# A streaming encoder block with mixture of experts: a new order of its front, 27 weight slots, sums in PSUM, late down biases, overflow loads on POOL's queue

## The chip, the cores and the metric

The kernel runs on one core of a Trainium2 chip. The metric is the device time of one execution in microseconds (us); a statement about a kernel rests on the median of its runs. Engines are named as in the profile: PE (TensorE), PEld (its weight loads), DVE (VectorE), ACT (ScalarE), POOL (GpSimd), SP (SyncE, which issues most DMA transfers here).

## What is computed

One block over 256 tokens of width 1024, float32: a projection, two attention mixers, a gated merge, a norm, then a mixture of 32 experts, four to a token, and a second norm.

```
proj = x @ w_in -> qa, ckv, qi, ki, wi, qb, kb, vb, ga, gb
y_a = sparse_indexed_attention(qa, rms_norm(ckv), qi, layer_norm(ki), wi, w_uk, w_uv)   # top 64 keys
y_b = chunk_band_attention(qb, kb, vb, rel_bias)
merged = sigmoid(ga) * (y_a @ w_branch_a) + sigmoid(gb) * (y_b @ w_branch_b)
x = layer_norm(DN_ALPHA * x + merged @ w_out)
logits = x @ w_router + b_router;  gates = softmax(top 4 of 32)
for each expert e and its tokens:
    h = (clip(x @ w_up[e] + b_up[e]) + 1) * swish(min(x @ w_gate[e] + b_gate[e], 7))
    y += gate * (h @ w_down[e] + b_down[e])
x = layer_norm(DN_ALPHA * x + y)
```

The weights of the experts are 3 x 4 MB each, so 12 loads of 1 MB to an expert and 384 of the kernel's 408 loads.

## The kernel before

**Slots.** SBUF is kept as 25 slots of 128 x 2048 float32 (1 MB). `slot()` takes one, `free()` and `done()` count it back; the buffer itself is free when the last reader has ended. All weights come through a list in the order of their use (L95 to L125): `load_next` (L78) takes a slot and issues one load on SP's queue, `pump(reserve)` (L86) issues loads as long as more than `reserve` slots stay free. SP issues in program order and waits at each load until its buffer is free. Beside the loads the slots hold x and its halves, scores, gates, and in the expert loop x1, wa, wb, wc (work tiles), acc (the sums) and, from the fourth to the 21st expert, the down biases.

**The front** (to L727). Products of the projections, branches and w_out run on halves: `ahead(n)` (L187) splits the first n chunks of 1 MB, each into a rounded high part (ACT, two activations) and the rest as low part (two subtractions on the engine that `LO_ENGINE` names, V for DVE or G for POOL), into two slots. `AHEAD` says how many chunks are split ahead of use and `RESERVE` what each pump leaves free. `project_T(g)` and `project(g)` run the three products of the halves for group g of two chunks; `used()` frees a chunk and pumps. The order before: B's queries and keys (groups 0, 1) with the indexer's scores and top-k on DVE, A's queries (2), B's scores and softmax, v of B (3), A's scores and softmax, gate A (4), `attend` B, gate A (5), `attend` A, gate B (6, 7), the branches A then B, w_out, norm, router. `exps` takes the maxima on DVE and the exponentials on ACT by head, `normalise` scales by head on DVE, `attend` turns the weights by PE transposes and then multiplies with v.

**The experts** (L931). For expert e: `run_gate_up(e)`, copies to SBUF, `run_down(e - 1)`, every second time the gather and gates of the next pair, `act_fn(e)`, and after every second expert `combine`, which multiplies a pair's rows back to the tokens in two fresh PSUM banks and adds them to acc on DVE. Four products open the sums in PSUM before the last expert (L963). `down_biases` (L895) runs at e = 3. At e = 20 `overflow` (L823) branches on the largest count of an expert's tokens; its body isn't entered with these inputs. The loads pumped behind the down of expert 19 go out on POOL's queue.

Of the kernel before, what the change touches and what calls it, by code (L numbers as in the profile page):

```python
# [15 lines left out]
NT = 2  # L16
D = 1024
KD = 8
H = 8
NE = 32  # L20
CAP = 64
TOPK = 64
# [26 lines left out]
def body(nc, tc, slots, sm, psp, xT_d, x_d, w_g0, w_qi, w_in, ikgb_d, wuk_d,  # L49
# [4 lines left out]
    # ---------------------------------------------------------------- slots and loads  # L54
# [42 lines left out]
    for i in range(2):  # L97
        plan(("ba", i), wba_d[i])
        plan(("bb", i), wbb_d[i])
# [27 lines left out]
    # ---------------------------------------------------------------- first loads  # L127
# [16 lines left out]
    ikgb = sm.tile([128, 3], F32, name="ikgb")  # L144
    SP.dma_start(ikgb, ikgb_d)
# [9 lines left out]
    epst = sm.tile([128, 1], F32, name="epst")  # L155
# [14 lines left out]
    # ---------------------------------------------------------------- exact halves of float32 operands  # L170
# [12 lines left out]
    order = [("in", i) for i in range(16)] + [("ba", 0), ("ba", 1), ("bb", 0), ("bb", 1)] + [("wo", i) for i in range(4)]  # L183
    IN, BA, BB, WO = 0, 16, 18, 20
    halves = []

    def ahead(n):  # L187
        """splits the first n chunks of that order"""
# [10 lines left out]
    def part(i, which, k, per):  # L199
        """row block k of chunk i"""  # L200
# [18 lines left out]
    def warm(n):  # L219
        """keeps the tensor engine's clock up while it waits"""  # L220
# [34 lines left out]
    def project(g, sink):  # L255
        """group g of the input projections, token-major"""
# [13 lines left out]
    def project_T(g, sink):  # L270
        """group g of the input projections, feature-major; two row blocks share a bank, so only the first starts it"""
# [21 lines left out]
    # k_idx layer norm and c_kv rms norm, token-major  # L293
# [26 lines left out]
    def head_scores(qT, kT, tb, sink):  # L320
        """pairs of heads lie on the two halves of the partitions"""
# [14 lines left out]
    # ---------------------------------------------------------------- B queries and keys, the indexer  # L336
# [51 lines left out]
    # ---------------------------------------------------------------- A queries  # L388
# [11 lines left out]
    V.memset(sB[1][0:64, :, 192:256], NEG)  # L400

# [3 lines left out]
    def exps(s, w, tb):  # L405
        V.tensor_reduce(mx[:, w, tb, :], s[tb], axis=AX.X, op=ALU.max, negate=True)
        for h in range(H):
            A.activation(s[tb][:, h, :], s[tb][:, h, :], AF.Exp, bias=mx[:, w, tb, h:h + 1],
                         accum_out=sums[:, w, tb, h:h + 1])

    def normalise(s, w, tb):
        V.reciprocal(sums[:, w, tb, :], sums[:, w, tb, :])
        for h in range(H):
            V.tensor_scalar(s[tb][:, h, :], s[tb][:, h, :], sums[:, w, tb, h:h + 1], None, op0=ALU.mult)
# [7 lines left out]
    for tb in range(NT):  # L422
        head_scores(qbT, lambda j: kbT[:, j, :], tb, score_sink(sB))
        exps(sB, 1, tb)
    free(1)
    sa0_s = slot("sa0_vb")
    sa1_s = slot("sa1")
    sA = [sa0_s[:, 0:1024].rearrange("p (h s) -> p h s", h=8), sa1_s.rearrange("p (h s) -> p h s", h=8)]
    for tb in range(NT):
        sl = slice(KOFF[tb], KOFF[tb] + KEYS[tb])  # L430
        for h in range(H):
            V.scalar_tensor_tensor(sA[tb][:, h, :], negd[:, sl], 2.0 ** -(h + 1), amask[:, sl],
                                   op0=ALU.mult, op1=ALU.add)
    free(1)
    vb = sa0_s[:, 1024:2048].rearrange("p (b c) -> p b c", b=2)
    project(3, lambda tb, p: acopy(vb[:, tb, :], p))
    normalise(sB, 1, 0)
    normalise(sB, 1, 1)
    for tb in range(NT):
        head_scores(qaT, lambda j: kaT[:, j, :], tb, score_sink(sA))  # L440
        exps(sA, 0, tb)
    free(2)

    y_s = [slot("yA"), slot("yB")]
    yHL = [[t[:, o:o + 1024].rearrange("p (j t) -> p j t", j=4) for o in (0, 1024)] for t in y_s]

    def attend(s, v, w):
        pts = [slot("pt0"), slot("pt1")]
        pT = [t[:, 0:1536].rearrange("p (b h t) -> p b h t", b=3, h=4) for t in pts]
        for j2 in range(2):  # L450
            for bi, (tb, sb) in enumerate(((0, 0), (1, 0), (1, 1))):
# [3 lines left out]
                (vcopy if bi != 1 else acopy)(pT[j2][:, bi, :, :].rearrange("p h t -> p (h t)"), p)  # L455
        for j2 in range(2):
            o = bank("pv")
            for jj in range(2):
                for tb in range(NT):
                    for sb in range(tb + 1):  # L460
                        for par in range(2):
# [3 lines left out]
                                      v[:, sb, h * 64:(h + 1) * 64], pT[j2][:, tb + sb, i, :],  # L465
                                      start=(sb == 0), stop=(sb == tb), skip_group_check=True)
            hi, lo = [t[:, 2 * j2:2 * j2 + 2, :] for t in yHL[w]]
# [3 lines left out]
    sg_s = [slot("sgA"), slot("sgB")]  # L471
    sg = [s.rearrange("p (k t) -> p k t", k=KD) for s in sg_s]

    def gate_sink(w, n):
        return lambda js, p: A.activation(sg[w][:, 4 * n + js.start:4 * n + js.stop, :], p, AF.Sigmoid)

    project_T(4, gate_sink(0, 0))
    attend(sB, vb, 1)
    free(2)
    normalise(sA, 0, 0)  # L480
    normalise(sA, 0, 1)
    project_T(5, gate_sink(0, 1))
    attend(sA, va, 0)
    free(3)
# [5 lines left out]
    mg = sg[1]  # L490
# [18 lines left out]
    yHL = [[t.bitcast(F32R) for t in hl] for hl in yHL]  # L509

    def branch(w, c, ps):
        """chunk c of a branch's rows; at the last one the gate and, for B, the sum of the two and its halves"""
        for f in range(KD):
# [10 lines left out]
            if w:  # L524
# [5 lines left out]
    for c in range(2):  # L530
        ahead(BA + c + 1 + AHEAD[BA + c])
        branch(0, c, ps)
# [5 lines left out]
    for c in range(2):  # L538
        ahead(BB + c + 1 + AHEAD[BB + c])
        branch(1, c, ps)  # L540
# [8 lines left out]
    def norm_apply(tb, groups):  # L549
        """z = (x1 - mean) * rstd, and x1 = z * g + b"""  # L550
# [38 lines left out]
    def route_sums(copy=vcopy):  # L589
        """the router's products by experts, in four sums over two row blocks each"""  # L590
# [7 lines left out]
    def route(tb):  # L598
        """the router's logits (the norm's gain in the weights, its offset in the row), and which experts a token takes"""
# [9 lines left out]
    def count_up(tb):  # L609
        """the place of each token among an expert's tokens; far off for the tokens that it doesn't take"""  # L610
# [11 lines left out]
    sgm = wa_s[:, 1536:1792].rearrange("p (j s) -> p j s", j=4)  # L622

# [38 lines left out]
    # the second token tile's last columns in two halves, for a shorter way from their sums to the norm  # L662
# [66 lines left out]
    # ---------------------------------------------------------------- experts  # L729
# [9 lines left out]
    def combine_weights(pt, gated):  # L739
        """pt = the gated one-hot rows turned, from their two halves of 64 columns for each token tile"""  # L740
# [6 lines left out]
    def dispatch_weights(g):  # L747
        """for the pair g of experts"""
# [39 lines left out]
    def down(hT, wd):  # L788
        """the halves of the columns on the halves of the partitions"""
# [7 lines left out]
    def rows_of(e, p, first=0, size=512):  # L797
        """an expert's rows to its half of the pair's partitions"""
# [3 lines left out]

    def combine(g):
# [7 lines left out]
    def add(tb, ps):  # L811
        for n in range(2):
# [273 lines left out]
```

## Time and profile before

| | us |
|---|---|
| three runs, median (lowest to highest) | 1157.8 (1157.16 to 1158.95) |
| span of the profiled execution | 1156.1 |
| PE busy in it | 1067.6 (92%) |
| DVE, ACT, POOL busy | 351.9, 227.6, 85.5 |
| moved by DMA | 437.51 MB, 378 GB/s on average |

The profile lists one execution. Busy shares are averages over stages with different limits; the stretches further down separate them. "Idle before ... <-X" names what ended an engine's idle time, a `q` behind an engine its instruction queue. L numbers are lines of the kernel before.

### The profile page before, as it was taken

To read this page: it belongs to the slowest core of one execution; us is meant where nothing else is said; L and a number is where in the kernel's file an instruction comes from. 1 tells how busy PE (TensorE), PEld (TensorE's weight loads), DVE (VectorE), ACT (ScalarE), POOL (GpSimd) and SP (SyncE) were. 2 spreads that over 40 slices of the span, in tenths; PEclk is the share of its full clock that TensorE was granted. 3 is DMA by queue.
4 is the path that set the end of the run, shared out by engine and by line. 5 is a ranking of instruction groups with operands and counts; after the bars stand their busy time and mean duration, and the time that the engine had idled before them with its cause. 6 is when DMAs were issued, how large, how long until landed. Compare 5 with 4: busy or idle time off the path is not lost. (4 is left out here: it accounts for less than half of the span.)

```text
span 1156.1 us, 13824 instructions
## 1 busy us (share of the span) xinstructions
PE 1067.6 (92%) x5599; PEld 540.9 (47%) x5599; DVE 351.9 (30%) x811; ACT 227.6 (20%) x424; POOL 85.5 (7%) x60
## 2 busy tenths in 40 slices
PE   8997899999899999999899999996699999999896
PEld 8987899634244443434343434341243434343432
DVE  6797826412212322121212121210212121212124
ACT  3645342221011111111111111110011111111112
POOL 4113723000000000000000000001000000000001
PEclk9997999999899999999999999998799999999998
DMA  8940747999999999999999999999989999999995
GB/s 335 382 154 1 280 180 306 359 420 422 407 405 421 421 420 421 421 421 421 421 421 421 421 422 421 421 422 422 418 353 421 421 421 421 421 421 421 421 421 189
DMA packets 63932, 437.51 MB, mean 378 GB/s; under 512 B 7252, under 2 KB 7892, under 8 KB 11892
## 3 DMA queue, kind: packets, MB, share of 16 engines
q1 hardware_dynamic: 61270, 421.61, 88.5%
q0 software_dynamic: 1728, 12.58, 2.6%
q10 hardware_dynamic: 864, 2.36, 0.6%
q8 instruction: 46, 0.75, 0.3%
q14 instruction: 24, 0.20, 0.0%
HBM read 435.48 MB, written 1.05 MB: 378 GB/s over the span
## 5 line engine op out<-in xcount | busy, mean ns | idle before, releaser
L761 PE MATMUL gu<-ld,wa 128*64 128x512 f32 x1024 | 458.9, 602 | 27.3 <-DMA ld<-in_dram 23.4
L759 PE MATMUL gu<-ld,wa 128*64 128x512 f32 x1024 | 457.9, 601 | 7.5 <-DVEq L832 6.8
L793 PE MATMUL y<-ld,wc 128*64 128x512 f32 x992 | 240.4, 606 | 19.7 <-DMA ld<-in_dram 19.7
L759 PEld LDWEIGHTS gu<-ld,wa 128*64 128x64 f32 x1024 | 136.7, 138 | 241.0 <-issue 221.4
L780 DVE TENSOR_TENSOR wc<-tr,wb 128x256 f32<-128x256 f32 x64 | 27.0, 422 | 669.7 <-PE tr L776 669.7
L761 PEld LDWEIGHTS gu<-ld,wa 128*64 128x64 f32 x1024 | 136.2, 138 | 93.2 <-DMA ld<-in_dram 46.4
L793 PEld LDWEIGHTS y<-ld,wc 128*64 128x64 f32 x992 | 77.4, 138 | 169.6 <-issue 131.2
L175 ACT ACTIVATE wb<-gu 128x512 f32<-128x512 f32 x64 | 38.3, 598 | 442.6 <-PE gu L761 234.5
L175 ACT ACTIVATE wc<-y 64x512 f32<-64x512 f32 (+1 forms) x66 | 38.3, 580 | 239.8 <-PE y L793 234.1
L279 PE MATMUL fm<-xh,hi 128*128 128x256 f32 x224 | 66.4, 297 | 9.7 <-ACT sa_vb L175 5.4
L635 PEld LDWEIGHTS ga<-wa,x 128*128 128x128 f32 x512 | 61.6, 196 | 12.4 <-issue 12.2
L180 POOL TENSOR_TENSOR lo<-ld,hi 128x1024 fp32r<-128x1024 f32 x24 | 59.0, 2491 | 97.7 <-ACT hi L175 72.4
L279 PE MATMUL fm<-xl,hi 128*128 128x256 f32 x224 | 65.2, 291 | 0.0
L279 PE MATMUL fm<-xh,lo 128*128 128x256 f32 x224 | 65.1, 291 | 0.0
L635 PE MATMUL ga<-wa,x 128*128 128x128 f32 x512 | 64.8, 285 | 0.0
L808 PE MATMUL c<-wc,wb 128*128 128x512 f32 x120 | 54.0, 592 | 0.0
L83 POOL DMA_DIRECT2D ld<-in_dram x12 | 6.7, 558 | 608.8 <-DMA ld<-in_dram 578.1
L175 ACT ACTIVATE hi<-ld 128x1024 fp32r<-128x1024 f32 x48 | 47.1, 1048 | 17.6 <-PE fm L279 8.8
L279 PEld LDWEIGHTS fm<-xh,hi 128*128 128x128 f32 x224 | 45.0, 201 | 10.9 <-ACT sa_vb L175 5.8
L279 PEld LDWEIGHTS fm<-xl,hi 128*128 128x128 f32 x224 | 45.0, 201 | 0.2 <-issue 0.2
L279 PEld LDWEIGHTS fm<-xh,lo 128*128 128x128 f32 x224 | 44.9, 200 | 0.0
L180 DVE TENSOR_TENSOR lo<-ld,hi 128x1024 fp32r<-128x1024 f32 x24 | 33.8, 1461 | 30.2 <-ACT hi L175 27.4
(244 smaller groups left out, 882.0 us busy)
## 6 DMA issues: line engine op xcount, KB each, us to landing
ld<-in_dram SPq DMA_DIRECT2D x392, 1024.0 KB, 19.8
ld<-in_dram POOLq DMA_DIRECT2D x12, 1024.0 KB, 25.0
ld<-in_dram SPq DMA_DIRECT2D x8, 512.0 KB, 14.2
wq<-in_dram ACTq DMA_DIRECT2D x3, 512.0 KB, 8.7
biasB<-in_dram SPq DMA_DIRECT2D x1, 1024.0 KB
x<-in_dram SPq DMA_DIRECT2D x1, 1024.0 KB
g<-in_dram SPq DMA_DIRECT2D x1, 800.0 KB, 9.7
xT<-in_dram SPq DMA_DIRECT2D x3, 256.0 KB, 6.9
```

What stands on the lines that cost most here:

```text
L83: eng.dma_start(part, from_)
L175: A.activation(o, i, AF.Copy)
L180: sub.tensor_tensor(lo.bitcast(F32R), t, hi, op=ALU.subtract)
L279: PE.matmul(ps[j // 2][:, j % 2 * 256:j % 2 * 256 + 256], part(i, b, k, 4)[:, j * 128:(j + 1) * 128], xHL[a][:, 4 * c + k, :], start=(c + ...
L635: PE.matmul(ps[j // per][:, (j % per) * n:(j % per + 1) * n], x1_cols(tb, j), Pt, start=(tb == 0 and j % per == 0), stop=(tb == 1), skip_g ...
L759: PE.matmul(ps[n][0:64, :], xe(j), wg(j, cs), start=(j == 0), stop=(j == KD - 1), skip_group_check=True)
L761: PE.matmul(ps[n][64:128, :], xe(j), wu(j, cs), start=(j == 0), stop=(j == KD - 1), skip_group_check=True)
L780: V.tensor_tensor(gg, pv[:, :, 0, :], bg(js), op=ALU.add)
L793: PE.matmul(p[64 * n:64 * n + 64, :], hT[:, j, :], wd(j, slice(n * 512, (n + 1) * 512)), start=(j == 0), stop=(j == KD - 1), skip_group_ch ...
L808: PE.matmul(ps[n], work["pt"][:, g % 2, tb, :], work["y"][:, n * 512:(n + 1) * 512], start=True, stop=True)
```

## The change

The front gets another order. The scores of A and B now each come behind a projection of a gate, the maxima, exponentials and scalings are separate steps, `normalise` is one tensor_tensor for each token tile instead of eight scalings, `attend` is split into `turn` (transposes) and `attend`, the gates of A are groups 3 and 4, v of B is group 5, branch B runs before branch A, and A's second half of attention runs inside branch B. The tables of reserves, lead and engines are new. The slots are 27, epst moves into ikgb and the area for software DMA descriptors shrinks to 1024. The sums of the experts' rows lie in four PSUM banks from the first expert on, opened by four products with a scaled identity; acc is gone from the loop and taken only at the end. The count of tokens stays at e = 3, the down biases are loaded at e = 26 and multiplied at e = 28, into the same sums. Overflow runs in a slot of its own; its loads, inside the branch, go out on POOL's queue, and the 12 loads of expert 19's pump on SP's. The host swaps two groups of columns to fit.

```diff
+OVERFLOW_AT = 20
+BD_AT = 26
-NSLOT = 25
+NSLOT = 27
-RESERVE = (8, 6, 5, 0, 4, 2, 5, 8, 3, 8, 1, 2, 3, 0, 8, 4, 3, 4, 1, 3, 5, 0, 0, 2, 0)
-AHEAD = (3, 4, 2, 4, 3, 3, 3, 3, 0, 0, 4, 3, 3, 4, 3, 2, 4, 3, 3, 2, 1, 4, 2, 0)
-LO_ENGINE = 'GVVGVVVVGGGGVGGGGVVGGVVV'
+RESERVE = (4, 3, 3, 3, 4, 5, 3, 3, 3, 1, 3, 3, 3, 2, 3, 1, 2, 4, 3, 1, 5, 1, 1, 1, 0)
+AHEAD = (3, 4, 3, 3, 3, 3, 3, 3, 3, 3, 3, 3, 3, 3, 3, 3, 3, 3, 3, 3, 3, 3, 2, 1, 0)
+LO_ENGINE = "GVVGGGGGGGGGGVGVGVGVGVVV"
...
+    def normalise(s, w):
+        V.reciprocal(sums[:, w], sums[:, w])
+        for tb in range(NT):
+            V.tensor_tensor(s[tb], s[tb], sums[:, w, tb, :, None].to_broadcast([128, H, KEYS[tb]]), op=ALU.mult)
...
+    project_T(3, gate_sink(0, 0))
+    for tb in range(NT):
+        head_scores(qbT, lambda j: kbT[:, j, :], tb, score_sink(sB))
+    maxima(sB, 1)
...
+    project_T(4, gate_sink(0, 1))
+    exps(sB, 1)
+    for tb in range(NT):
+        head_scores(qaT, lambda j: kaT[:, j, :], tb, score_sink(sA))
+    maxima(sA, 0)
+    project(5, lambda tb, p: acopy(vb[:, tb, :], p))
+    normalise(sB, 1)
+    exps(sA, 0)
+    turn(sB, 1)
+    project_T(6, gate_sink(1, 0))
+    attend(vb, 1)
+    normalise(sA, 0)
+    project_T(7, gate_sink(1, 1))
+    turn(sA, 0)
...
+        branch(1, c, ps)
+        if c == 0:
+            attend(va, 0)
...
+    def summed(tb, n, lhsT, rhs, start=False, stop=False):
+        PE.matmul(sums[tb][n], lhsT, rhs, start=start, stop=stop, skip_group_check=True)
+    def open_sums():
+        V.tensor_scalar(identa, ident, ALPHA, None, op0=ALU.mult)
+        for tb in range(NT):
+            for n in range(2):
+                summed(tb, n, identa, x1[:, tb, n * 512:(n + 1) * 512], start=True)
     def combine(g):
         for tb in range(NT):
-            ps = [bank("c0"), bank("c1")]
             for n in range(2):
-                PE.matmul(ps[n], work["pt"][:, g % 2, tb, :], work["y"][:, n * 512:(n + 1) * 512], start=True, stop=True)
-            add(tb, ps)
+                summed(tb, n, work["pt"][:, g % 2, tb, :], work["y"][:, n * 512:(n + 1) * 512])
...
-                            SP.dma_start(ow, src[col, j // 2, :, o + cs.start:o + cs.stop]
+                            G.dma_start(ow, src[col, j // 2, :, o + cs.start:o + cs.stop]
...
-        pump(0, G if e == 19 else SP)
+        pump(1 if e in (OVERFLOW_AT - 2, OVERFLOW_AT - 1, BD_AT - 2, BD_AT - 1) else 0)
...
-            ov_s = down_biases()
+            count()
...
-            overflow(ov_s)
+        if e == OVERFLOW_AT:
+            overflow(slot("ov"))
+        if e == BD_AT:
+            bd_s = slot("bd")
+            SP.dma_start(bd_s[0:NE, 0:1024], bd_d)
+        if e == BD_AT + 2:
+            down_biases(bd_s)
...
-    nc = _bacc.Bacc("TRN2", target_bir_lowering=False, num_devices=1)
+    nc = _bacc.Bacc("TRN2", target_bir_lowering=False, num_devices=1, dynamic_dma_scratch_size=1024)
```

## Rows read from the trace of the kernel before

**Rows 1.** The page's chain of work that ended last, by engine.

```profile
DMA 18%; PE 7%; DVE 1%; SPq 0%; issue 0%; DVEq 0%
```

**Rows 2.** Stretches: length, each engine's busy time, PE's clock, DMA share, GB/s.

```profile
0.00:140.00 140.00, 122.60 (x938) 114.25 (x939) 112.15 (x207) 69.16 (x137) 52.20 (x31) 0.94 0.58 224
140.00:300.00 160.00, 158.82 (x1024) 105.33 (x1024) 57.87 (x125) 39.79 (x63) 21.47 (x14) 1.00 0.85 346
300.00:340.00 40.00, 36.57 (x158) 15.24 (x156) 8.12 (x22) 5.14 (x11) 0.00 (x0) 0.87 0.99 398
340.00:820.00 480.00, 444.33 (x2052) 180.91 (x2048) 99.17 (x269) 66.26 (x126) 6.69 (x12) 0.99 1.01 421
820.00:860.00 40.00, 30.56 (x130) 12.50 (x131) 2.88 (x8) 2.98 (x5) 0.00 (x0) 0.83 0.91 372
1120.00:1157.00 37.00, 25.59 (x140) 10.73 (x136) 13.46 (x26) 7.76 (x14) 5.15 (x3) 0.89 0.59 229
```

**Rows 3.** The chain in order of time: start, length (us), what.

```profile
900.15 19.81 DMA ld<-in_dram
...
1108.38 3.70 PE sum L963 x8
```

**Rows 4.** PE's gate products (L759): least, median, most ns; first and last start.

```profile
L759 PE MATMUL gu<-ld,wa x1024: 592/592/1115, 221.0 to 1125.4; 128*64 128x512 f32 x171
```

**Rows 5.** Groups on PE, 60 to 186 us: busy, mean ns, idle before.

```profile
L279 PE MATMUL fm<-xh,hi 128*128 128x256 f32 x150 | 44.9, 299 | 9.7 <-ACT sa_vb L175 5.4 <-DVE sa_vb L419 4.2
...
L464 PE MATMUL pv<-pt,uku 128*64 128x128 f32 x48 | 4.6, 371 | 1.9 <-DVE pt L172 1.9
L464 PE MATMUL pv<-pt,sa_vb 128*64 128x128 f32 x48 | 2.8, 275 | 0.0
...
L454 PE MATMUL ptr<-ident,sa 128*128 128x128 f32 x16 | 2.5, 285 | 1.9 <-DVE sa L414 1.9
```

**Rows 6.** Stretches for line L279 alone: PE, PEld, granted clock, DMA share, GB/s.

```profile
90.00:95.00 5.00, 4.93 (x24) 4.73 (x24) 0.59 0.01 3
99.00:110.40 11.40, 11.15 (x72) 10.94 (x72) 0.77 0.00 0
115.60:127.50 11.90, 11.77 (x96) 11.56 (x96) 1.00 0.86 328
```

**Rows 7.** ACT: exponentials of B, a table load, high halves.

```profile
L408 ACT ACTIVATE biasB<-biasB,mx x16: 389/452/497, 78.6 to 85.1; 128x128 f32<-128x128 f32 x8, 128x256 f32<-128x256 f32 x8
...
77.28 1.28 ACT L408 ACT_TABLE_LOAD   x1 [8.78 <-DVE mx L406]
...
L175 ACT ACTIVATE hi<-ld 128x1024 fp32r<-128x1024 f32 x48 | 47.1, 1048 | 17.6 <-PE fm L279 8.8
```

**Rows 8.** Groups: DVE and POOL 60 to 165 us; the x12 row, DVE 17 to 49.

```profile
L414 DVE TENSOR_SCALAR sa_vb<-sa_vb,sums 128x128 f32<-128x128 f32 x8 | 11.8, 1545 | 0.0
...
L414 DVE TENSOR_SCALAR biasB<-biasB,sums 128x256 f32<-128x256 f32 x8 | 2.2, 350 | 0.0
...
L180 DVE TENSOR_TENSOR lo<-ld,hi 128x1024 fp32r<-128x1024 f32 x4 | 4.7, 1220 | 5.5 <-ACT hi L175 5.5
...
L180 DVE TENSOR_TENSOR lo<-ld,hi 128x1024 fp32r<-128x1024 f32 x12 | 19.7, 1702 | 5.7 <-ACT hi L175 5.7
...
L180 POOL TENSOR_TENSOR lo<-ld,hi 128x1024 fp32r<-128x1024 f32 x16 | 37.8, 2393 | 67.7 <-ACT hi L175 42.4 <-DVE misc L383 23.4 <-issue 1.9
```

**Rows 9.** SP's queue: its wait at the branch; its issues before and after.

```profile
SPq L832 <- SPq L832: 36.9, 6, 13.6
...
800.73 5.29 SPq L83 DMA_DIRECT2D ld<-in_dram  x2
...
844.18 15.21 SPq L83 DMA_DIRECT2D ld<-in_dram  x13
```

**Rows 10.** The products of the down biases on PE.

```profile
L908 PE MATMUL bd<-bd 32*128 32x512 f32 x8 | 7.2, 1072 | 3.4 <-DMA bd<-in_dram 3.4
```

**Rows 11.** The page's group of copies that empty a bank.

```profile
L175 ACT ACTIVATE wb<-gu 128x512 f32<-128x512 f32 x64 | 38.3, 598 | 442.6 <-PE gu L761 234.5
```

More of the change, by code (lines that the diff above doesn't have):

```diff
@@ L97, in body @@
     for i in range(2):
+        plan(("bb", i), wbb_d[i])
+    for i in range(2):
         plan(("ba", i), wba_d[i])
-        plan(("bb", i), wbb_d[i])
     for i in range(4):
@@ L180, in split @@
         sub.tensor_tensor(lo.bitcast(F32R), t, hi, op=ALU.subtract)
-    order = [("in", i) for i in range(16)] + [("ba", 0), ("ba", 1), ("bb", 0), ("bb", 1)] + [("wo", i) for i in range(4)]
-    IN, BA, BB, WO = 0, 16, 18, 20
+    order = [("in", i) for i in range(16)] + [("bb", 0), ("bb", 1), ("ba", 0), ("ba", 1)] + [("wo", i) for i in range(4)]
+    IN, BB, BA, WO = 0, 16, 18, 20
     halves = []
@@ L400, in body, with maxima, exps @@
     V.memset(sB[1][0:64, :, 192:256], NEG)
+    sg_s = [slot("sgA"), slot("sgB")]
+    sg = [s.rearrange("p (k t) -> p k t", k=KD) for s in sg_s]
     mx = sm.tile([128, 2, NT, H], F32, name="mx")
     sums = sm.tile([128, 2, NT, H], F32, name="sums")
[L405 to L414, printed above, removed]
+    def maxima(s, w):
+        for tb in range(NT):
+            V.tensor_reduce(mx[:, w, tb, :], s[tb], axis=AX.X, op=ALU.max, negate=True)
+    def exps(s, w):
+        for tb in range(NT):
+            for h in range(H):
+                A.activation(s[tb][:, h, :], s[tb][:, h, :], AF.Exp, bias=mx[:, w, tb, h:h + 1],
+                             accum_out=sums[:, w, tb, h:h + 1])
+    def normalise(s, w):
+        V.reciprocal(sums[:, w], sums[:, w])
+        for tb in range(NT):
+            V.tensor_tensor(s[tb], s[tb], sums[:, w, tb, :, None].to_broadcast([128, H, KEYS[tb]]), op=ALU.mult)
     def score_sink(s):
@@ L420, in score_sink, with gate_sink, turn @@
         return sink
[L422 to L449, printed above, removed]
+    def gate_sink(w, n):
+        return lambda js, p: A.activation(sg[w][:, 4 * n + js.start:4 * n + js.stop, :], p, AF.Sigmoid)
+    y_s = [None, None]
+    yHL = [None, None]
+    pts = [None, None]
+    def turn(s, w):
+        pts[w] = [slot("pt0"), slot("pt1")]
         for j2 in range(2):
+            pT = pts[w][j2][:, 0:1536].rearrange("p (b h t) -> p b h t", b=3, h=4)
             for bi, (tb, sb) in enumerate(((0, 0), (1, 0), (1, 1))):
@@ L530, in body @@
     for c in range(2):
-        ahead(BA + c + 1 + AHEAD[BA + c])
-        branch(0, c, ps)
+        ahead(BB + c + 1 + AHEAD[BB + c])
+        branch(1, c, ps)
+        if c == 0:
+            attend(va, 0)
+            free(1)
     free()
@@ L538, in body @@
     for c in range(2):
-        ahead(BB + c + 1 + AHEAD[BB + c])
-        branch(1, c, ps)
+        ahead(BA + c + 1 + AHEAD[BA + c])
+        branch(0, c, ps)
     free(3)
@@ L866, in overflow @@
                     for tb in range(NT):
-                        cps = [bank("c0"), bank("c1")]
                         for n in range(2):
                             h = slice(64 * n, 64 * n + 64)
-                            PE.matmul(cps[n], opt[h, tb, :], y[h, :], start=True, stop=True)
-                        add(tb, cps)
+                            summed(tb, n, opt[h, tb, :], y[h, :])
     def open_work():
@@ L893, in gates, with down_biases @@
             V.tensor_scalar(gt[:, tb, :], gt[:, tb, :], nm[:, tb, 2:3], None, op0=ALU.mult)
[L895 to L897 removed]
+    def down_biases(bd_s):
         gT = bd_s[0:NE, 1024:1024 + T]
         bd = bd_s[0:NE, 0:1024]
[L900 removed]
         p = bank("gT")
@@ L906, in down_biases, with count @@
             for n in range(2):
-                p = bank("bd")
-                PE.matmul(p, gT[:, tb * 128:(tb + 1) * 128], bd[:, n * 512:(n + 1) * 512], start=True, stop=True)
-                cs = slice(n * 512, (n + 1) * 512)
-                V.tensor_tensor(acc[:, tb, cs], acc[:, tb, cs], p, op=ALU.add)
+                summed(tb, n, gT[:, tb * 128:(tb + 1) * 128], bd[:, n * 512:(n + 1) * 512])
+    def count():
         p = bank("cnt")
@@ L925, in run_down @@
         done(4)
-        pump(0, G if e == 19 else SP)
+        pump(1 if e in (OVERFLOW_AT - 2, OVERFLOW_AT - 1, BD_AT - 2, BD_AT - 1) else 0)
         rows_of(e, p)
-    acc = None
+    sums = [[bank("sum") for _ in range(2)] for _ in range(NT)]
     last = NE - 1
@@ L934, in body @@
             open_work()
-            acc_s = slot("acc")
-            acc = acc_s.rearrange("p (b c) -> p b c", b=2)
             gates()
@@ L954, in body @@
             combine(e // 2 - 1)
-        if e == 20:
-            overflow(ov_s)
+        if e == OVERFLOW_AT:
+            overflow(slot("ov"))
             free()
-    sums = [[bank("sum") for _ in range(2)] for _ in range(NT)]
-    for tb in range(NT):
-        for n in range(2):
-            PE.matmul(sums[tb][n], ident, acc[:, tb, n * 512:(n + 1) * 512], start=True, stop=False,
-                      skip_group_check=True)
+        if e == BD_AT:
[3 more added lines that the diff above has]
+            down_biases(bd_s)
+            free()
     evac_gu(run_gate_up(last))
@@ L968, in body @@
     run_down(last - 1)
-    ln2_s = slot("ln2")
+    ln2_s, acc_s = slot("ln2"), slot("acc")
+    acc = acc_s.rearrange("p (b c) -> p b c", b=2)
     SP.dma_start(ln2_s[0:1, :], ln2_d)
@@ L1053 @@
         w[:, :, ranges(2)].transpose(1, 0, 2),
-        chunks(ranges(5, 6, 0, 7, 8, 9)),
+        chunks(ranges(5, 6, 0, 8, 7, 9)),
         np.stack([np.tile(a["idx_k_norm_g"][0], 2), np.tile(a["idx_k_norm_b"][0], 2), a["kv_norm_g"][0]], axis=1),
```

59 lines of the change are left out of this document (30 added, 29 removed).

## The prediction

> **What bounds the kernel now.** I read three views first. The chain of work that ended last gives 18% of the span to DMA and 7% to PE [rows 1]: it ends in transfers that follow each other. The stretches [rows 2] say how long this has held: from 340 to 820 us the DMA moves 421 GB/s at a share of 1.01, so it is full, while PE is busy for 444 of 480 us. A load of 1 MB (the slot's 1024 KB) lands 19.8 us after its issue with eight under way [rows 3], 2.48 us each; twelve loads to an expert make 29.8 us, and PE's work on one is at most 444 x 29.8 / 480 = 27.6 us [rows 2]. So in the experts only time in which the DMA stands idle counts. All 437.5 MB of the page at 421 GB/s take 1039 us; the rest of the 1156 is DMA time lost, and [rows 2] say where, each as length x (1 - GB/s / 421): 0 to 140 us 65.5, 140 to 300 us 28.5 (together 94 in and just behind the front), 300 to 340 us 2.2, 820 to 860 us 4.7, from 1120 us on 17. Of that last 17 the output and the second norm are most, and no edit takes them off.
>
> Why is the DMA idle in the front? It can't run further ahead than there are slots: a load needs a free one of 25. When the first expert starts at 221.0 us [rows 4] every slot is full, and from then on PE frees them faster than the DMA fills them. The lost time is therefore (start of the first expert) minus (bytes that fit by then) / 421 GB/s, and only two things change it: an earlier start, or more slots filled by it.
>
> **The change, part by part.**
> *Two more slots.* I counted slots in the order of the code: at the last pump of the front x1 and wa are held, so before it 25 - 2 = 23 expert loads are out and after it 27 - 2 = 25. A slot of 1 MB is one load. Two more by the same point are 2 x 2.48 = **5.0 us** [rows 3] less to load behind it. The front has 94 us of idle DMA to take them in. acc and the slot of the down biases no longer stay; the DMA is full by then, so I count nothing for these two, which would cost nothing if missing.
>
> *The new order of the front.* PE waits in it for 5.4 and 4.2 us (for the softmax of branch B and the scores of A), then 1.9 and 1.9 us (normalised A, its turned weights) [rows 5]: 13.4 us. Around these waits its granted clock is 0.59 and 0.77, between the levels of 1.2 and 2.4 GHz, and behind idle time: 24 products of a projection take 4.93 us and 72 take 11.15, where 96 at clock 1.00 take 11.77 [rows 6], so 2.0 + 2.3 us are lost; the second attend takes 4.6 us where the first takes 2.8 [rows 5], 1.8 more. Together 13.4 + 6.1 = **19.5 us** is what the front can give. The new order puts a projection of 11.8 us between each step of the softmax and PE's use of it: gate A's before and after the scores of B, v's after the scores of A, gate B's between turn and the other attend.
>
> What is late next? Taken from the end of project_T(4): ACT, in order, has a sigmoid (0.6, as a copy of the same size [rows 11]), a table load (1.3), the exponentials of B (first to last 7.0) and then the high halves of chunk 13 (two of 1.0) [rows 7], so at 11 us DVE gets chunk 13 (now "V") and by 12.3 starts normalise(sB). PE has the scores of A (about 3 us, an estimate from 24 products in 2.9 us) and v (11.8, the same number of columns as a projection) and wants sB turned at 14.8. The two tensor_tensor of normalise are 1024 and 2048 columns wide, 1.2 and 2.4 us by the size of a lone subtraction [rows 8], so alone they end at 16.1, and PE stands for 1 to 2 us. But POOL starts the low halves of chunk 14 at 12 to 13, two of 2.4 us [rows 8]. The rows show what then happens: eight small scalings of 128 columns took 11.8 us, 1545 ns each, beside POOL's subtractions, where scalings twice as wide took 350 ns; and subtractions on DVE took 1702 ns on average where POOL ran, 1220 where it didn't [rows 8]. One DVE instruction and one of POOL take turns. So each of the two waits for one of POOL's: 2 x 2.4 = 4.8 us, and normalise ends at 21. PE, which has the first four transposes done, loses 6 us there, and 2 more by its clock, as behind the wait of 5.4 us [rows 5, 6]: **8 us**. Bounds: 0 (nothing of it shows) to 19.5 (the waits come back elsewhere); I take 8, the sum of its own rows. The Trainium skill's page "SBUF — State Buffer", section "Who interferes with whom", says it as a rule: DVE and GpSimd share one pair of ports under an exclusive lock, and a tensor_tensor whose two inputs lie in SBUF takes part in it against a GpSimd read. It speaks against this part of the change, since a trace in which only the scalings took turns would leave the new normalise free; then the stall would be 1.3 us, hardly a clock lost, and the time 6 us lower. By the rule it is the forecast's, and the rows of the subtractions are on its side.
> The same turn-taking hits the 16 steps that build A's distances (DVE, two SBUF inputs), which now may run beside POOL's chunks 11 and 12: at most two chunks, 4 x 2.4 us. They are wanted only by the scores of A, whose banks are read 11 us later, under v's projection: nothing on PE's path, but without that cover up to 10 us. POOL has 15 chunks in place of 12, 4.8 us each [rows 8] against 5.9 us that PE spends on one [rows 6], split three chunks ahead: hidden. Later turns (sA) have a whole projection of cover. Front: 19.5 - 8 = **11.5 us**.
>
> *Overflow loads on the POOL queue.* At the branch SP waits 36.9 us in six waits for its own transfers to land; its last load before is issued by 806 us and the next at 844.2 [rows 9]. This drains the DMA: 4.7 us lost [rows 2]. Afterwards SP issues nothing inside the branch. POOL, which issues nothing in it now, passes it with 12 loads of its own under way and without such waits, so I expect SP to do the same: **4.7 us**, bounds 0 to 4.7. POOL then waits in SP's place, with nothing queued behind it before the last broadcast. The 12 loads go back to SP; the DMA is full either way: 0.
>
> *Late down biases.* At the fourth expert PE waits 3.4 us for the biases and runs their products in 7.2 us [rows 10], DVE adds four times, and the slots of the next down come free late: 2.2 us lost from 300 to 340 us [rows 2]. Late in the loop PE waits for weights anyway. **2.1 us**, with 0 to 2.2 as bounds; their own transfer stays.
>
> *Sums in PSUM.* 64 additions of DVE go, none on the path; eight products that opened the sums before the last expert (3.7 us [rows 3]) move to the first. There they push the second expert's gate and up, and so its slots, by 3.7 us, at a point where the DMA has the six loads of the first pump in hand (14.9 us) against a gate and up, half or more of PE's 27.6: I charge **1 us** (0 to 3.7). What it gives at the end is nothing: the last transfers land later than PE.
>
> Sum: 11.5 + 5.0 + 4.7 + 2.1 - 1.0 = 22.3 us. The span of 1156.1 becomes 1133.8; the median of the runs is 1.7 us above the span, so **1135.5 us**.
>
> **The rivals.**
> *The front gives little.* ACT's order (exponentials ahead of the halves and of turn's copies) and the turns with POOL cost more than 8 us, and PE stands again in the projections of gate B. For it: ACT has some 30 us of work in a row there. Against: every product has a chunk of cover. If 9 more are lost, 1144.5 (1140 to 1151). Chance 0.15.
> *SP still drains at the branch*, because the waits belong to every engine and not to the issuer. Then 4.7 more: 1140. Against: POOL's passage. Chance 0.08.
> *All waits of the front close*: 8 less, 1127.5. Chance 0.07.
> *Slower: the banks.* The sums hold four of the eight PSUM banks through the whole expert loop. Gate and up, down, turns and gather share four, so a product can wait for the copy that empties its bank. Six copies or reads of a bank belong to an expert (two each of gu, y and tr), 0.6 us each [rows 11]; exposed in full they make 3.6 us. It decides once PE's 27.6 us grow beyond the DMA's 29.8; with 22 us in hand, 0.7 for each of 31 experts, the kernel is slower than before beyond 30.5, 2.9 us an expert more. All 3.6 exposed: (31.2 - 29.8) x 31 = 43 us, about 1179. Against it: in the order of allocation each bank's reader has a whole down or gate and up to finish. Chance 0.03.
>
> **How the numbers follow.** Forecast 1135.5, own range 1130 to 1140, chance 0.66; the other four as above, 0.01 for the rest. The range 1127 to 1145 leaves out the slow end of the first rival and the banks. A measurement tells 0.2% (2.3 us) from no change. Faster: all but the banks and what is left, 0.95; same 0.02; slower 0.03.
>
> **What would show it.** First gu product at about 209.5 us; clock 1.00 from 60 to 140 us but for one wait at the transposes of sB, ended by DVE's normalise with POOL beside it; 25 expert loads issued by then; no dip below 415 GB/s near the branch and at 300 us; PE's waits in the loop still for DMA alone. The forecast is wrong if the first expert starts after 215 us, if SP's issues stop at the branch, or if PE waits in the loop for ACT or DVE.

## The result, and the profile after

The changed kernel takes 1138.6 us (median of four runs, 1137.62 to 1139.6) against 1157.84 for the kernel before: a ratio of 0.9833, 95% interval 0.9819 to 0.9847. The forecast was 1135.5 in a range of 1127 to 1145, so the direction and the range hold, and the gain is 3.1 us smaller than the sum said (19.2 for 22.3). The profiled execution took 1137.62, the shortest of the four, with a span of 1136.0: 20.1 us less than the span before.

Stretches of the changed kernel (length, each engine's busy time, PE's granted clock, DMA share, GB/s), in the cuts of [rows 2] and three narrower ones:

```profile
0.00:140.00 140.00, 130.58 (x1005) 122.87 (x1006) 89.36 (x164) 73.69 (x142) 74.83 (x39) 0.96 0.65 255
140.00:300.00 160.00, 158.87 (x1002) 97.94 (x1003) 59.25 (x134) 37.70 (x61) 16.58 (x12) 1.00 0.89 358
300.00:340.00 40.00, 40.00 (x200) 17.30 (x198) 9.42 (x28) 6.70 (x13) 0.00 (x0) 1.00 1.01 421
340.00:820.00 480.00, 446.81 (x2093) 183.97 (x2090) 75.51 (x224) 66.13 (x126) 0.00 (x0) 0.99 1.01 421
820.00:860.00 40.00, 38.68 (x176) 14.10 (x176) 9.42 (x28) 4.85 (x10) 0.00 (x0) 1.00 1.01 421
...
110.00:120.00 10.00, 4.90 (x29) 4.57 (x30) 7.94 (x6) 8.31 (x36) 3.49 (x2) 0.66 0.04 5
...
230.00:240.00 10.00, 10.00 (x50) 3.34 (x48) 3.27 (x11) 0.42 (x1) 0.00 (x0) 1.00 0.93 351
...
1000.00:1020.00 20.00, 16.58 (x72) 5.19 (x68) 0.11 (x1) 1.19 (x2) 0.00 (x0) 1.00 1.02 403
```

Counted as in the prediction, length x (1 - GB/s / 421), the DMA now loses 55.2 us up to 140 us and 23.9 from there to 300: 79.1, where it lost 94.0. The 2.2 at 300 to 340 and the 4.7 at 820 to 860 are gone. New is 0.9 at 1000 to 1020, where the down biases are loaded now; the 1.7 at 230 to 240 is part of the 79.1. So 14.9 + 2.2 + 4.7 - 0.9 = 20.9 us, close to the 20.1 of the spans. Both kernels move the same 437.5 MB, so the lost time of the whole span has to differ by as much as the spans do; what the count shows is where it differs (the rates are whole GB/s, and half of one is 0.6 us of a stretch of 480).

PE's longest waits over the whole span (us in total, times, longest):

```profile
PE gu L777 <- DMA ld<-in_dram: 28.9, 28, 1.4
PE y L809 <- DMA ld<-in_dram: 16.3, 34, 1.0
PE ptr L446 <- DVE biasB L423: 5.7, 2, 3.5
PE gu L775 <- PEq L851: 3.8, 1, 3.8
PE gu L775 <- issue: 3.2, 1, 3.2
```

PE's gate products (least, median, most ns; first and last start):

```profile
L775 PE MATMUL gu<-ld,wa x1024: 592/592/1116, 209.9 to 1102.5; 128*64 128x512 f32 x171
```

The first expert starts at 209.9 us where it started at 221.0 [rows 4]. In the loop PE waits for weights, and at the branch (3.8 us, and 3.2 five us behind it, for which the profile shows no cause). Of the front's four waits [rows 5] none is left; the one that the prediction set in their place, at the transposes of sB, is there. This is what DVE and POOL do around it (start, length, what), and the groups that answer [rows 5]:

```profile
108.15 7.48 DVE L423 TENSOR_TENSOR biasB<-biasB,sums 128x1024 f32<-128x1024 f32 x2
107.53 5.96 POOL L183 TENSOR_TENSOR lo<-ld,hi 128x1024 fp32r<-128x1024 f32 x2 [9.26 <-ACT hi L178]
```

```profile
L446 PE MATMUL ptr<-ident,biasB 128*128 128x128 f32 x24 | 4.5, 364 | 5.7 <-DVE biasB L423 5.7
L462 PE MATMUL pv<-pt,sa_vb 128*64 128x128 f32 x48 | 2.8, 275 | 0.0
L462 PE MATMUL pv<-pt,uku 128*64 128x128 f32 x48 | 2.8, 275 | 0.0
L446 PE MATMUL ptr<-ident,sa 128*128 128x128 f32 x16 | 2.1, 273 | 0.0
```

DVE's two multiplications lie beside POOL's two subtractions and end 2.1 us after these; the transposes behind them take 364 ns where the later ones take 273, at a granted clock of 0.66 from 110 to 120 us, between its two levels (1.2 and 2.4 GHz), behind PE's wait. Both attends now take 2.8 us.

At the branch, SP's waits from 780 to 860 us:

```profile
SPq L85 <- DMA ld<-in_dram: 66.5, 32, 2.7
```

The instructions of the branch's line, where POOL and SP pass it:

```profile
L851 POOLq COMPARE_BRANCH  x1: 45/45/45, 295.2 to 295.2; - x1
L851 SPq COMPARE_BRANCH  x1: 50/50/50, 815.1 to 815.1; - x1
```

The wait of 36.9 us [rows 9] is gone: SP's waits there are those ahead of its loads, ended by landings of other loads, 2.7 us at the most. POOL passes the branch at 295 us, 490 us ahead of PE, since nothing of its own lies before it.

### The profile page after: what moved, and what is told of

It is laid out like the page before. It is cut to its first block, busy times and chain, and to the rows that moved or that the text cites. A ratio compares the mean times of both kernels' runs of the same rounds, so it can differ in the third digit from the quotient of the medians.

```text
span 1136.0 us, 13723 instructions
## 1 busy us (share of the span) xinstructions
PE 1061.2 (93%) x5599; PEld 535.3 (47%) x5599; DVE 293.4 (26%) x711; ACT 228.7 (20%) x425; POOL 96.6 (9%) x54
## 3 DMA queue, kind: packets, MB, share of 16 engines
q10 hardware_dynamic: 864, 2.36, 0.6%
## 5 line engine op out<-in xcount | busy, mean ns | idle before, releaser
L183 POOL TENSOR_TENSOR lo<-ld,hi 128x1024 fp32r<-128x1024 f32 x30 | 76.5, 2575 | 62.6 <-ACT hi L178 50.3
L984 POOL PARTITION_BROADCAST ln<-ln x1 | 2.3, 2298 | 929.0 <-DMA ld<-in_dram 929.0
L821 PE MATMUL sum<-wc,wb 128*128 128x512 f32 x120 | 54.0, 592 | 0.0
L798 ACT ACTIVATE wa<-wc 128x256 f32<-128x256 f32 x64 | 26.6, 416 | 79.4 <-DVE wc L797 78.8
```

Source lines behind the costliest of these rows:

```text
L798: A.activation(sg_, gg, AF.Sigmoid, scale=1.702)
L821: PE.matmul(sums[tb][n], lhsT, rhs, start=start, stop=stop, skip_group_check=True)
L984: G.partition_broadcast(ln2_s, ln2_s[0:1, :])
```

## Experiments

Each kernel below was timed five times or more beside the kernel before. The interval of a ratio reaches 0.0013 to 0.0021 either way, 1.5 to 2.4 us, so a difference below 2 us rests on the trace, not on the medians alone. The changed kernel itself was run again, as the reference for three kernels below: the old form of normalise, the biases left out, and the combination with ACT.

> The changed kernel as it is, as the common reference of the other kernels of this call. Every theory: 1138.6 us within 1; what it differs from that is how far the medians of two calls can be compared.

Measured: 1138.72 us (1136.98 to 1140.6), 0.12 from the first. Its profiled execution starts the first expert at 211.7 us, 1.8 later than the one above, with the clock at 0.92 from 120 to 132 us where that has 1.00. That clock is only part of it: PE comes to the transposes of sB 0.7 us later already, and the rest is added behind its wait. Other kernels below whose front is the same start the first expert between 208.1 and 211.5 us, so the front varies by 2 us in one program and by 3.6 over these kernels.

**The wait at the transposes of sB.**

```
-AHEAD = (3, 4, 3, 3, 3, 3, 3, 3, 3, 3, 3, 3, 3, 3, ...)
+AHEAD = (3, 4, 3, 3, 3, 3, 3, 3, 3, 3, 3, 2, 3, 3, ...)
```

> The changed kernel, with chunk 14 of the front split one chunk later (the twelfth entry of AHEAD is 2 in place of 3), so that POOL has no subtraction while DVE normalises sB. Theory (DVE and POOL take turns, and that is why normalise ended late): normalise(sB) takes 3.4 us in place of 7.48, the two waits of PE at the transposes of sB (5.7 us together) shrink to one of at most 1.8, the first gate product comes at 203 to 205 us in place of 209.9, and the time falls by the same amount, to 1132 to 1134 us. Rival (ACT's order makes normalise late, the turns with POOL are a side effect): the waits stay above 4 us and the time within 2 us of 1138.6. Second rival (PE starts earlier but the slots aren't filled by then): first gate product near 204, time above 1136.

Measured: 1133.38 us (0.9785, 0.9768 to 0.9802), 5.2 less than the changed kernel. Normalise in the timeline:

```profile
107.20 3.43 DVE L423 TENSOR_TENSOR biasB<-biasB,sums 128x1024 f32<-128x1024 f32 x2
```

PE's wait at the transposes:

```profile
PE ptr L446 <- DVE biasB L423: 1.6, 1, 1.6
```

The gate products:

```profile
L775 PE MATMUL gu<-ld,wa x1024: 592/592/1085, 205.1 to 1100.8; 128*64 128x512 f32 x171
```

The same two multiplications take 3.43 us in place of 7.48 once POOL's subtractions are elsewhere, and the first expert starts 4.8 us earlier, earlier than in any kernel with the changed kernel's front (208.1 at the least). ACT's two high halves of that chunk moved too; that acts on when normalise starts (107.20 for 108.15), not on how long its instructions last. The first theory holds, with its numbers (the first expert comes 0.1 us behind its 203 to 205). The turns themselves haven't gone; they have moved under cover. POOL's subtractions now start at 118.08 us, and DVE's two of another chunk, 2.36 us by themselves, take 5.00 beside them while PE waits for neither:

```profile
119.93 5.00 DVE L183 TENSOR_TENSOR lo<-ld,hi 128x1024 fp32r<-128x1024 f32 x2 [4.70 <-ACT hi L178]
```

**What takes turns: the old form of normalise, in the changed kernel.**

```
-            V.tensor_tensor(s[tb], s[tb], sums[:, w, tb, :, None].to_broadcast(...), op=ALU.mult)
+            for h in range(H):
+                V.tensor_scalar(s[tb][:, h, :], s[tb][:, h, :], sums[:, w, tb, h:h + 1], None, op0=ALU.mult)
```

> The changed kernel with the normalisation of a softmax in the old form, a scaling for each head (16 instructions) in place of two multiplications. Theory (DVE's instructions with both ends in SBUF take turns with POOL's, whatever their kind): the 16 scalings, 4.8 us without POOL, are held up by POOL's two subtractions of chunk 14, up to 6 us in all, so normalise(sB) takes 9 to 11 us in place of 7.5, PE waits 2 to 4 us longer for the transposes of sB, and the time is 1140.5 to 1142.5. Rival (only the multiplications with two inputs take turns, the scalings go on beside POOL): normalise(sB) about 5 us, PE's wait 2 to 3 us shorter, 1135.5 to 1136.5.

Measured: 1136.01 us (0.9815, 0.9801 to 0.9829), 2.7 below the reference. The theory fails. The rival's time holds (1135.5 to 1136.5), but not its mechanism, as the lengths show. Normalise and POOL in the timeline:

```profile
107.63 7.70 DVE L424 TENSOR_SCALAR biasB<-biasB,sums 128x128 f32<-128x128 f32 x16
107.02 4.96 POOL L183 TENSOR_TENSOR lo<-ld,hi 128x1024 fp32r<-128x1024 f32 x2 [8.98 <-ACT hi L178]
```

The lengths of normalise's instructions (least, median, most ns):

```profile
L424 DVE TENSOR_SCALAR biasB<-biasB,sums x16: 274/341/2384, 107.6 to 115.0; 128x128 f32<-128x128 f32 x8, 128x256 f32<-128x256 f32 x8
```

PE's waits at the transposes (L447 here):

```profile
PE ptr L447 <- DVE biasB L424: 2.0, 1, 2.0
PE ptr L447 <- PE tm L267: 1.0, 1, 1.0
PE ptr L447 <- PE ptr L447: 0.8, 1, 0.8
```

The scalings wait too, so the rival falls: two of them last 2124 and 2384 ns, as long as one of POOL's, and fourteen run at 274 to 343. So it is POOL's instructions that set the price, one of DVE's for each of them: with two on POOL, 16 scalings take 7.70 and two multiplications 7.48. My 9 to 11 added the 6 us to the scalings' whole time, though two of the scalings run within it. The kernel before shows the same count behind the mean of 1545 ns in [rows 8]:

```profile
114.31 14.20 POOL L180 TENSOR_TENSOR lo<-ld,hi 128x1024 fp32r<-128x1024 f32 x6 [18.18 <-ACT hi L175]
L414 DVE TENSOR_SCALAR sa_vb<-sa_vb,sums x8: 274/2103/2455, 117.4 to 128.9; 128x128 f32<-128x128 f32 x8
```

Of these eight scalings five last 1798 to 2455 ns, one beside each of the five subtractions that POOL runs meanwhile, and the three that come after POOL's last take 274 to 275. Of B's first eight there, four are long, beside four subtractions. PE waits 3.8 us in place of 5.7, because the scaled heads come one by one; the two long instructions of the changed kernel hand over 8 heads at a time. The trace gives 1.9 us for that wait. Whether the time gained is more than the front's own variation isn't shown: the first expert starts at 207.9 us, just below the 208.1 to 211.7 of the same front with multiplications.

**The opening of the sums.**

```
-        if e == 0:
-            open_sums()
...
+        if e == 2:
+            open_sums()
```

> The changed kernel, with the eight products that open the sums moved from the first expert to the third, just before the first combine. Theory (opened in the first expert they hold up the second expert's products, and the DMA runs out of issued loads between 230 and 240 us, where it moves 351 GB/s): the dip goes, 1.6 us come back, about 1137.0 us. Rival (the dip comes from the start of the loop itself, the first pump's six loads, whatever PE does there): the dip stays and the time is the changed kernel's 1138.6 within 0.5.

Measured: 1136.97 us (0.9816, 0.9798 to 0.9833), 1.6 less. Two stretches of 10 us:

```profile
230.00:240.00 10.00, 10.00 (x50) 3.40 (x48) 1.62 (x6) 0.00 (x0) 0.00 (x0) 1.00 1.02 427
290.00:300.00 10.00, 10.00 (x48) 3.42 (x50) 0.00 (x0) 0.00 (x0) 0.00 (x0) 1.00 0.96 390
```

The dip at 230 us goes with the products, so they are its cause; a smaller one, 0.7 us, comes at 290 us. In the trace these two slices gain 1.0, in the medians it is 1.6. This profiled execution is the slowest of its five (1138.85, first expert at 211.5 us). The dip differs between executions too: 0.9 to 1.7 us in the others that open the sums in the first expert, 0.4 with the late chunk 14.

**The overflow loads**, from both sides: back on SP in the changed kernel, and on POOL's queue in the kernel before (with its twelve loads ahead of the branch on SP).

```
-                            G.dma_start(ow, src[col, j // 2, ...
+                            SP.dma_start(ow, src[col, j // 2, ...
```

> The changed kernel, with the overflow loads inside the branch issued by SP again. Theory (the queue whose loads stand inside the branch is waited empty ahead of it, whoever it is): SP stops issuing some 30 us before the branch, the DMA dips there to about 370 GB/s in one slice of 40 us, and the time rises by 4.7 us to 1143.3. Rival (the dip of the kernel before came from its twelve loads on POOL's queue or from the kernel's place in the loop): no dip, 1138.6 within 1.

> The kernel before with one part of the change alone: the overflow loads on POOL's queue and the twelve loads ahead of the branch back on SP. Theory: SP passes the branch without waiting, the 4.7 us that the DMA loses there come back whole, since it is full on both sides of the branch: 1157.8 becomes 1153.1. Rival (the lost transfers are made up by the slots' cushion before the end): 1157.8 within 1.

Measured: 1141.23 (0.9857, 0.9839 to 0.9874), 2.6 above the changed kernel; and 1153.51 (0.9966, 0.9953 to 0.9979), 4.1 below the kernel before. The changed kernel with SP, a stretch and SP's wait:

```profile
800.00:840.00 40.00, 36.78 (x188) 16.71 (x186) 4.30 (x12) 5.87 (x11) 0.00 (x0) 1.00 0.90 370
```

```profile
SPq L851 <- SPq L851: 18.5, 4, 11.1
```

The kernel before with POOL, the same two views:

```profile
820.00:860.00 40.00, 40.00 (x204) 17.43 (x201) 5.98 (x17) 7.47 (x14) 0.00 (x0) 1.00 1.01 421
```

```profile
SPq L83 <- DMA ld<-in_dram: 64.3, 31, 3.2
```

The wait and the dip follow the queue whose loads stand inside the branch. 4.8 us are lost in the first, none in the second. The times are 1141.2 for 1143.3 expected, and 1153.5 for 1153.1. That only 2.6 of the 4.8 show in the first's median (3.9 in its profiled execution) is within what two medians differ by. The tail makes up none of it: from the last load's landing to the end are 15.2 us, and 15.3 in the changed kernel.

**Two slots fewer.**

```
-NSLOT = 27
+NSLOT = 25
```

> The changed kernel with 25 slots in place of 27, all else as it is. Theory (the DMA's lost time is the start of the first expert less the bytes that fit into the slots by then): the first gate product stays near 209.9 us, two loads fewer are out by then, and 5.0 us more are lost by 220 us: 1143.6 us. Rival (the reserves of each pump are written for 27 slots, and with 25 the front's own chunks come late): the first gate product moves behind 212 us and the time rises by 7 us or more. Second rival (the two slots are given back in the loop, where loads wait for others anyway): within 1 us of 1138.6.

Measured: 1142.58 (0.9875, 0.9853 to 0.9896), 4.0 more. Its stretches up to 300 us:

```profile
0.00:140.00 140.00, 130.31 (x1002) 122.71 (x1003) 88.32 (x164) 73.38 (x141) 74.95 (x39) 0.98 0.62 240
140.00:300.00 160.00, 158.87 (x1003) 98.10 (x1003) 59.54 (x134) 37.93 (x61) 16.59 (x12) 1.00 0.89 359
```

Its gate products:

```profile
L775 PE MATMUL gu<-ld,wa x1024: 592/592/1061, 210.2 to 1108.9; 128*64 128x512 f32 x171
```

The first expert starts when it did; 83.8 us are lost up to 300 us where it was 79.1, 4.7 more. Two loads of 2.48 us are what the slots hold, so the theory holds. (The profiled execution is the second slowest of its five, 6.2 us longer than the changed kernel's.)

**The down biases**: back in the fourth expert, and left out.

```
-        pump(1 if e in (OVERFLOW_AT - 2, OVERFLOW_AT - 1, BD_AT - 2, BD_AT - 1) else 0)
+        pump(1 if e in (OVERFLOW_AT - 2, OVERFLOW_AT - 1) else 0)
...
         if e == 3:
             count()
+            bd_s = slot("bd")
+            SP.dma_start(bd_s[0:NE, 0:1024], bd_d)
+            down_biases(bd_s)
+            free()
...
-        if e == BD_AT:
-            bd_s = slot("bd")
-            SP.dma_start(bd_s[0:NE, 0:1024], bd_d)
-        if e == BD_AT + 2:
-            down_biases(bd_s)
-            free()
```

The kernel without the biases lacks the four added lines from `bd_s` on as well.

> The changed kernel with the down biases loaded and multiplied in the fourth expert, as in the kernel before, their products now going into the sums in PSUM. Theory (their place costs what the DMA loses there): the 2.2 us between 300 and 340 us come back as a loss, and the 0.8 to 1.0 us that the changed kernel loses at 1010 to 1020 us, where it loads them now, go: 1139.7 us. Rival (late they cost nothing, as the prediction has it): 1140.7. Second rival (the sums in PSUM, without DVE's additions, had removed the loss already): 1138 or less.

> The changed kernel without the load of the down biases and their products (this part of the computation is left out). Theory (late they cost the dip of the DMA at 1000 to 1020 us, 1.0 us, and their products nothing): 1137.6 us, and no dip there. Rival (the dip is made up at the end, where PE waits for the last loads anyway, so that late they cost nothing): the reference's 1138.6 within 0.4. Second rival (the slot that they keep free for two experts costs as well, 2.5 us a load): 1136.1 or less.

Measured: 1137.88 early (0.9821, 0.9802 to 0.9841), 0.7 *below* the changed kernel, and 1137.26 without (0.9823, 0.9807 to 0.9838), 1.5 below its reference of 1138.72. Early, the time is that of the second rival (1138 or less); without, it is nearest the theory's 1137.6, but both rivals lie within 1.4 of it. Stretches of the first, one of the second, then two of the kernel before:

```profile
290.00:300.00 10.00, 6.23 (x26) 2.14 (x23) 1.15 (x6) 1.45 (x3) 0.00 (x0) 0.87 1.01 365
320.00:330.00 10.00, 10.00 (x50) 3.60 (x51) 4.30 (x12) 1.04 (x3) 0.00 (x0) 1.00 0.99 405
```

```profile
1000.00:1020.00 20.00, 17.74 (x78) 5.92 (x76) 1.13 (x3) 1.32 (x3) 0.00 (x0) 1.00 1.01 422
```

```profile
300.00:310.00 10.00, 6.57 (x17) 2.37 (x14) 1.08 (x2) 1.45 (x3) 0.00 (x0) 0.79 1.01 381
330.00:340.00 10.00, 10.00 (x48) 3.30 (x46) 0.86 (x3) 0.20 (x1) 0.00 (x0) 1.00 0.92 370
```

Early they lose 1.3 + 0.4 = 1.7 us, late 0.9: by the traces the move gains 0.8, by the medians it loses 0.7, so nothing that these runs can tell from zero. Without load and products there is no dip, and the changed kernel shows which of the two makes it (the load's issue, then the products):

```profile
L972 SPq DMA_DIRECT2D bd<-in_dram x1: 331/331/331, 996.2 to 996.2; - x1
L821 PE MATMUL sum<-bd x8: 587/587/1052, 1027.2 to 1030.6; 32*128 32x512 f32 x8
```

The load is issued at 996.2 us and lands 18.9 us later, the dip lies between 1000 and 1020, and the products come behind it. So the load costs about 1 us wherever it stands, though its 0.13 MB (32 rows of 4 KB) are 0.3 us at 421 GB/s. The kernel before has two dips: 0.95 us around the load's landing and 1.2 about 20 us behind the products. With the sums in PSUM the second is down to 0.4 in the same place, so most of it went without the move. That DVE's four additions were its cause isn't shown: nothing here takes them out alone.

**The order of the front alone** (with the sums in PSUM): 25 slots, overflow loads on SP, biases early, three of the edits above together.

> The changed kernel with three parts undone together: 25 slots, overflow loads on SP, down biases in the fourth expert. What is left of the change is the new order of the front and the sums in PSUM. Theory (the parts add up): the prediction's 11.5 less 1.0 makes 1147.3 against the kernel before at 1157.8; from the traces, 15.2 us of DMA time less lost behind the front, less 5.0 for two slots, make 10.2, so 1147.6. Rival (the new order pays only with the two slots that take in what it frees): 1152 or more. Second rival (the slots are worth nothing by themselves, the order all of it): 1143 or less.

Measured: 1146.68 (0.9906, 0.9889 to 0.9924), 11.1 below the kernel before; the sum had 11.5 - 1.0 = 10.5, so the theory holds. From here to the changed kernel are 8.1 us; the three parts undone one by one give 4.0 + 2.6 - 0.7 = 5.9, so they add up to within the medians' scatter, and the order doesn't need the slots to pay. The 11.1 isn't the front's alone: the trace loses 11.8 us less up to 300 us and 2.0 less from 300 to 340, and 1.6 more at the branch.

**Put together**: the late chunk 14, the sums opened in the eleventh expert, the transposes taken by token tile; then the same with ACT issuing the load of the biases.

```
-AHEAD = (3, 4, 3, 3, 3, 3, 3, 3, 3, 3, 3, 3, 3, 3, ...)
+AHEAD = (3, 4, 3, 3, 3, 3, 3, 3, 3, 3, 3, 2, 3, 3, ...)
...
-        for j2 in range(2):
-            for bi, (tb, sb) in enumerate(((0, 0), (1, 0), (1, 1))):
+        for bi, (tb, sb) in enumerate(((0, 0), (1, 0), (1, 1))):
+            for j2 in range(2):
...
-        if e == 0:
-            open_sums()
...
+        if e == 10:
+            open_sums()
```

The products of the first `combine` now start the banks, which the opening did before.

> The changed kernel with chunk 14 of the front split one chunk later, the sums opened in the eleventh expert (the first combine starts the banks in their place), and the transposes of a softmax taken by token tile first, so that eight in place of four need only the first of normalise's two multiplications. Theory: 5.2 us for the chunk (as measured by itself), 1.6 us for the sums, since PE waits for weights by then, and up to 0.5 us of the remaining wait of 1.6 at the transposes of sB: 1131.3 us, with no dip of the DMA below 400 GB/s from 210 to 300 us beyond the pump's own at 220. Rival (what the sums cost is only moved, as from the first to the third expert, where 0.7 us showed again): 1132.5 to 1133.5.

> The combination of before (chunk 14 split one chunk later, the sums opened in the eleventh expert, the transposes by token tile) with the load of the down biases issued by ACT in place of SP. Theory (the 1.0 us that the DMA loses at 1000 to 1010 us come from the small load taking one of the places that SP's queue keeps under way): the dip goes, 1129.3 us against 1130.3. Rival (the loss is the transfer's own, 32 rows of 4 KB): the dip stays, 1130.3 within 0.5.

Measured: 1130.26 (0.9756, 0.974 to 0.9772) and 1129.2 (0.9753, 0.9739 to 0.9766). Stretches of the one, then of the other:

```profile
230.00:240.00 10.00, 10.00 (x49) 3.28 (x47) 0.49 (x2) 1.47 (x3) 0.00 (x0) 1.00 1.01 420
...
1000.00:1010.00 10.00, 7.96 (x35) 2.59 (x33) 0.00 (x0) 1.20 (x2) 0.00 (x0) 1.00 1.00 377
```

```profile
990.00:1000.00 10.00, 9.10 (x48) 7.27 (x50) 2.82 (x9) 4.04 (x8) 0.00 (x0) 0.71 1.01 400
1000.00:1010.00 10.00, 10.00 (x50) 3.39 (x48) 1.48 (x5) 0.42 (x1) 0.00 (x0) 1.00 1.02 423
```

The first lies 1.0 below its theory, the second at its theory's 1129.3, though the dip is still there. Opened late the sums cost nothing that shows. The biases' dip of 1.0 us shrinks to 0.5 on ACT's queue, so half of it was the place on SP's queue at most; the medians can't settle a half microsecond. Both kernels beat the changed one, by 8.3 and 9.5 us.

## Why the prediction was right, step by step

*What bounds.* Only time with an idle DMA counts: the 20.9 us lie where the prediction looked for them, and the larger parts undone moved the time by about the DMA time that their traces lost (4.0 for 4.7, 5.2 for 5.4, 4.1 for 4.7; the overflow loads put back gave 2.6 for 4.8).

*The front, 11.5.* Right: first gate product at 209.9 for 209.5 predicted, 25 expert loads issued by then for 25, the order with the sums worth 10.5 predicted and 11.1 measured. That it is 0.4 us off is in part luck, as the same front starts the expert between 208.1 and 211.7. *Its stall, 8.* The mechanism is right in each link: normalise was 4.05 us longer than alone for 4.8 predicted, PE waited 5.7 for 6, the clock fell behind it. To remove the turns gave 5.2, where the prediction put 6 on them: a wait of 1.6 stays for 1.3 predicted, since normalise alone (3.43) is longer than its cover, and a lower clock with it (346 ns a transpose in that kernel). The prediction took all eight scalings at 1545 ns for the price; the trace has five long and three short ones, as many long ones as POOL had subtractions beside them, which the 2 x 2.4 had right. The Trainium skill's page "SBUF — State Buffer", section "Who interferes with whom", says that whoever issues first has the shared pair for the whole instruction and the other is blocked. The trace agrees: each long multiplication took 1.9 to 2.2 us more than alone, beside subtractions of 2.4. It also names tensor_scalar, the form of the scalings, among the operations that can contend, under conditions. Here two of 16 did, at 2124 and 2384 ns.

*Two slots, 5.0.* Right: 4.0 by the median, 4.7 in the trace up to 300 us.

*Overflow loads, 4.7.* Right in the kernel before (4.1) and in the changed kernel's trace (4.8; 2.6 by the median). Two details were wrong. When POOL passed the branch of the kernel before at 815 us, six of its 12 loads were under way, not all. And POOL didn't wait in SP's place: it had no transfer under way and passed at once.

*Late down biases, 2.1.* This is the term that was mis-sized. I took 2.1 of the 2.2 us lost from 300 to 340 us as the price of the place, which leaves 0.1 for the load's own transfer. About 1 us is the load's own and went along with it, so from the kernel before to the changed one the traces gain 2.2 - 0.9 = 1.3. Not all of this is the move's: with the sums in PSUM the early place loses 1.7 us, so the move itself is worth 0.8 by the traces (0.2 against the kernel with the front alone, which loses 1.1 there), and the medians don't show even that. The term accounts for 0.8 of the 2.2 us by which the span's gain (20.1) fell short of 22.3. The front, slots and sums together account for 0.6 (15.5 predicted, 14.9 in the trace), and the rest isn't placed.

*Opening the sums, -1.0.* About right: 1.7 in this trace, 0.9 to 1.7 in the others, 1.6 by the median. Two experts later the trace shows 0.7, ten later nothing.

*The rivals.* Of SP's drain, the banks and a front that gives little, none shows, and that all waits of the front close is ruled out by the 5.7 us at sB. PE waits in the loop for no copy but one of 0.5 us at the biases, which by the letter of the last sign is a wait for ACT. How near the four remaining banks are to the limit wasn't tried.

## What to carry to other kernels

Where transfers bound a kernel, count idle DMA time by stretch and price each edit by the stretch that it touches; a dip holds the cost of a load's place and of the load, and a move recovers only the first. When DVE work on the path runs beside GpSimd, count GpSimd's instructions in that window: moving those away gave more than recasting DVE's. Keep loads that stand inside a branch off the queue that feeds the loop.

## What the runs showed of the hardware that I had not expected

- A queue without transfers under way passed a branch that holds its loads 490 us before PE (POOL at 295 us); the one that feeds the loop waited 18.5 and 36.9 us there.
- A load of 0.13 MB among loads of 1 MB cost a full DMA 0.9 to 1.0 us, three times its bytes; issued on ACT's queue 0.5, in one trace.
- A short DVE instruction that met one of POOL's waited as long as a long one (2384 ns, where 274 is the least), and only one did for each of POOL's: two of 16 beside two subtractions, five of eight beside five. So 16 scalings and two multiplications took 7.70 and 7.48 us beside the same two subtractions.
- The same program's first expert started at 209.9 and 211.7 us in two executions: 0.7 us of this were there before PE's wait at sB, the rest came behind it, where the clock was 1.00 in the one and 0.92 in the other from 120 to 132 us.
